# Eight long-convolution products: two channel tiles by turns, one written order for four engines, filter spectra re-indexed through DRAM

## The chip, the core and the metric

One core of a Trainium2 chip runs the kernel. The metric is the device time of one execution in microseconds (us), lower is better. The engines are named as in the profile: PE (matmuls; PEld its weight loads), DVE (VectorE), ACT (ScalarE), POOL (GpSimd), SP (its queue issues most of the DMAs; ACT's queue issues some).

## What is computed

One layer of a hybrid encoder on 2048 tokens of width 1024, in float32. One input projection feeds two mixers. The change is in the first, a gated long convolution over the whole sequence with filters that a small network makes from positions:

```python
def long_conv(z, h_fwd, h_bwd, d_skip):
    L = z.shape[1]
    n = 2 * L
    zf = jnp.fft.rfft(z, n=n, axis=1)
    hf = jnp.fft.rfft(h_fwd, n=n, axis=0) + jnp.conj(jnp.fft.rfft(h_bwd, n=n, axis=0))
    y = jnp.fft.irfft(zf * hf[None], n=n, axis=1)[:, :L]
    return y + z * d_skip

def hyena_mixer(u, ...):
    v, x1, x2 = jnp.split(short_conv3(u, conv_w, conv_b), 3, axis=-1)
    h = hyena_filters(L, ...)
    z = x1 * long_conv(v, h[:, 0, 0], h[:, 0, 1], sk[0])
    z = x2 * long_conv(z, h[:, 1, 0], h[:, 1, 1], sk[1])
    return z
```

There are 512 channels, so four tiles of 128, and two convolutions in series for each: eight products. The second mixer is a recurrence (RWKV-7). Both mixers are then projected, gated and merged, and a dense channel mixer (SwiGLU) follows.

## The kernel before

The stages in order of time: the input projection with the preparation of the recurrence, the recurrence (`chain`, L622) with the rest of the projection beside it, the convolutions (`hyena`, L1230), the merging of the mixers (`merge`, L1470) and the channel mixer (`ffn`, L1619). The change is in `hyena` and in what hands over to it at both ends.

A convolution of a tile of 128 channels goes through an FFT in two steps. `turned` (L1240) transposes the input on PE so that time lies on partitions. `fwd` (L1253) is the first step, matmuls with `Fz` into the tile `U`. `flip` (L1221) swaps indices inside SBUF with four 32x32 block transposes of 128x1024 on DVE, from `U` to `V`. `step3` (L1274) is the second step, matmuls with `Mc` into the PSUM tile `pz`; eight blocks q = 0 to 7 make a tile. For blocks 1 to 7 of the data `parts` (L1264) first splits `V` into a high and a low part `vh` (ACT and DVE), and three float32r matmuls of 512 columns replace the four float32 matmuls of 128. The two lines at L1317 and L1318 then multiply `pz` by the filter's spectrum `H` and by `Hs` (the same with real and imaginary blocks swapped, made by four small DMAs at L1290). `back` (L1297) adds the two products up with eight matmuls (`pq`) and ACT copies them to `Q` (L1304). `flip` turns `Q` into `V` again, `inverse` (L1327) is the last step, `po`. After the first convolution of a tile the result is multiplied by `x1` (L1394) and goes on to `fwd`; after the second `finish` (L1335) transposes it back (`pv`) and gates it with `x2` (L1343).

The filters go the same way: `filt` (L1184) makes, for each of eight blocks, the taps (`pg`, L1206), multiplies them by a window (four ACT exponentials, L1205; DVE, L1210), transforms them (`pf`, L1196) and copies them to `U` (L1197); sixteen pieces of four matmuls per filter. `flip` makes `Vf` of it, and `load` (L1283) its spectrum `H`. `short` (L1157) makes the rows `v`, `x1` and `x2` by a three-tap convolution, in four blocks (ACT L1171, DVE L1172 and L1177).

The eight products run tile by tile (c = 0 to 3), the two of a tile one after the other. PE's order is the order in which the code is written (`manual_schedule` for PE alone); the other engines are ordered by a scheduler, with `high_priority` marks. A product is written as a loop over q in which pieces of the next filter are pulled in (`share`); between two products stand the flips, the inverse, the gate and the next forward transform. After the last product stand the weights of the other mixer's output (`branch_weights`) and seven of its blocks (`right`).

Of the kernel before, what the change touches and what calls it, by code (L numbers as in the profile page):

```python
# [37 lines left out]
TB = 256  # L38

# [149 lines left out]
class Layer:  # L189
# [38 lines left out]
    def build(self):  # L228
        tc, nc = self.tc, self.nc
        with tc.tile_pool(name="dr", bufs=1, space=DRAM) as dr, tc.tile_pool(name="keep", bufs=1, reuse_waits="tile") as keep:  # L230
# [8 lines left out]
            self.Yd = T("Yd", [NCH, P, 256])  # L239
            self.Nd, self.Wd = T("Nd", [2, P, 1024]), T("Wd", [2, P, 1024])  # L240
# [378 lines left out]
    def ring(self, k, n=512):  # L619
        return self.cm.tile([P, 514], F32, name="rg", tag=f"rg{k % 14}")[:, 0:n]  # L620

    def chain(self):  # L622
# [3 lines left out]
        with tc.tile_pool(name="ch", bufs=1, reuse_waits="tile") as s, tc.tile_pool(name="chp", bufs=1, space=PSUM, reuse_waits="tile") as ps:  # L626
# [316 lines left out]

            LAST = N - 3
# [87 lines left out]
            with tc.manual_schedule(engines={mybir.EngineType.PE}):  # L1032
# [17 lines left out]
                taps, pieces = iter(()), [1, 2, 3]  # L1050
                self.rush = 0
                for n in range(N):
# [5 lines left out]
                    if n == LAST + 1:  # L1058
                        taps = self.filt(0, 0)
# [27 lines left out]
                self.taps = taps  # L1087
# [8 lines left out]
    def part(self, gen, need):  # L1096
        while need > 0:
            t = next(gen, None)
            if t is None:
                return  # L1100
            need -= t
            yield t


    def open(self):
# [3 lines left out]
        cu = self.wp.tile([P, 1024], F32, name="cu0", tag="wraw", bufs=2)  # L1109
# [3 lines left out]
        self.turns = dict(cu=0, row=0, w=0, g=0, A=0, B=0, H=0, Hs=0)  # L1113
        self.smalls, self.Vfs = {}, {}
# [4 lines left out]
        self.small(0, 0)  # L1119
        self.taken(0)  # L1120
        self.cus = [cu, self.ring(13, 514)]
        self.z0 = self.short(0, True)
# [12 lines left out]
    def next(self, name):  # L1135
        first, n = dict(w=(8, 2), g=(10, 2), A=(12, 2), B=(0, 2), H=(2, 3), Hs=(5, 3))[name]
# [15 lines left out]
    def row(self):  # L1152
        self.turns["row"] += 1
        return self.cm.tile([P, L], F32, name="co", tag=f"X{1 - self.turns['row'] % 2}")


    def short(self, ct, byrest):  # L1157
        nc, cw, cb = self.nc, self.cw, self.cb
        stt = nc.vector.scalar_tensor_tensor
        o = self.row()  # L1160
        for b in range(NB):
            u = self.cus[self.turns["cu"] % 2]
            self.turns["cu"] += 1
# [5 lines left out]
            nc.sync.dma_start(u[:, lo:hi], self.ud[ct, :, 512 * b - 1 + lo:512 * b - 1 + hi])  # L1169
# [14 lines left out]
    def filt(self, c, o):  # L1184
# [3 lines left out]
        if (c, o) != (HT - 1, 1):  # L1188
            self.small(c + o, 1 - o)
# [530 lines left out]
```

## Time and profile before

| | us |
|---|---|
| median of 3 runs | 3982.31 (3978.8 to 3995.08) |
| the profiled execution | 3993.76, of it 3992.0 from the first to the last instruction |
| projection and recurrence, to PE's last projection matmul | 0 to 1546 |
| end of the recurrence | 1546 to 1600 |
| convolutions, to the last added product | 1600 to 2128 |
| their end, to the first merging matmul | 2128 to 2148 |
| merge and channel mixer | 2148 to 3992 |

A row of the view of stretches gives for each engine the busy time and in brackets the instructions; a float32 matmul of PE is recorded as two. PEclk is the clock that PE was granted, as a share of 2.4 GHz; its other level is 1.2 GHz. In the view of groups, behind the bar stands the idle time of the engine just before the group's instructions, with what ended it.

### The profile page before, as it was taken

What the parts mean: (1) busy time and instruction counts of PE and PEld (TensorE: products, weight loads), DVE (VectorE), ACT (ScalarE), POOL (GpSimd) and SP (SyncE); (2) the same over time, 40 slices, a digit from 0 to 9 for tenths busy, and PEclk for the clock granted to TensorE, in tenths of its full rate; (3) what the DMA queues carried; (4) which work ended last, traced back from release to release, by engine and by line L of the source; (5) the groups of instructions that cost most, each with busy time, mean ns of one, the idle gap of its engine ahead of it and who ended that gap; (6) DMA issues with size and microseconds to landing.
All of it is one profiled execution on the core that took longest, in us unless ns stands there. A gap on an engine that the chain in (4) does not pass through costs nothing. (4 is left out here: it accounts for less than half of the span.)

```text
span 3992.0 us, 64401 instructions
## 1 busy us (share of the span) xinstructions
PE 3822.1 (96%) x25872; PEld 3128.8 (78%) x25872; DVE 2420.1 (61%) x3823; ACT 1488.8 (37%) x2914; POOL 93.1 (2%) x139
## 2 busy tenths in 40 slices
PE   8999999999999998898998999999999999999998
PEld 6766557787787777787887999788888878888887
DVE  4456884666667774878776655544444474444444
ACT  3345663333345567565654332211111151111113
POOL 0000001111010100000000000000000000000000
PEclk9999999999999999899999999999999999999999
DMA  4566878677777775221225433411111132111111
GB/s 139 173 167 172 221 208 245 203 220 208 218 225 224 214 193 178 63 77 46 81 63 176 131 122 117 164 48 48 48 48 48 48 134 78 48 48 48 48 48 43
DMA packets 389554, 501.84 MB, mean 126 GB/s; under 512 B 135220, under 2 KB 270909, under 8 KB 388549
## 3 DMA queue, kind: packets, MB, share of 16 engines
q1 hardware_dynamic: 362631, 443.13, 37.5%
q10 hardware_dynamic: 20736, 37.80, 3.1%
q0 software_dynamic: 5888, 16.78, 1.5%
q8 instruction: 204, 3.34, 0.4%
q14 instruction: 95, 0.78, 0.1%
HBM read 352.74 MB, written 127.93 MB: 120 GB/s over the span
## 5 line engine op out<-in xcount | busy, mean ns | idle before, releaser
L201 PE MATMUL acc<-xh,wh 128*128 128x512 f32 x1376 | 580.2, 422 | 10.3 <-ACT xh L196 9.2
L202 PE MATMUL acc<-xl,wh 128*128 128x512 f32 x1376 | 549.3, 399 | 6.6 <-DVE xl L197 4.9
L203 PE MATMUL acc<-xh,wl 128*128 128x512 f32 x1376 | 548.8, 399 | 0.5 <-DVE wl L197 0.5
L1657 DVE TENSOR_TENSOR acc<-pd,acc 128x1024 f32<-128x1024 f32 x320 | 387.8, 1222 | 70.9 <-PE pd L203 65.1
L196 ACT CAST fwh<-raw 128x1024 fp32r<-128x1024 f32 x132 | 138.6, 1050 | 705.0 <-PE pg L202 488.0
L201 PEld LDWEIGHTS acc<-xh,wh 128*128 128x128 f32 x1376 | 262.9, 191 | 122.9 <-issue 48.2
L1685 DVE TENSOR_TENSOR h<-pu,sg 128x512 f32<-128x512 f32 x88 | 60.9, 692 | 483.1 <-PE pu L203 475.8
L202 PEld LDWEIGHTS acc<-xl,wh 128*128 128x128 f32 x1376 | 263.3, 191 | 65.5 <-DVE xl L197 7.9
L203 PEld LDWEIGHTS acc<-xh,wl 128*128 128x128 f32 x1376 | 262.7, 191 | 65.1 <-issue 1.9
L201 PE MATMUL pd<-fwh,hh 128*128 128x512 f32 x704 | 276.8, 393 | 2.0 <-DVE acc L1655 1.6
L201 PE MATMUL pu<-fxh,fwh 128*128 128x512 f32 x704 | 276.2, 392 | 0.4 <-ACT fxh L1571 0.4
L201 PE MATMUL pg<-fxh,fwh 128*128 128x512 f32 x704 | 276.6, 393 | 0.0
L203 PE MATMUL pg<-fxh,fwl 128*128 128x512 f32 x704 | 275.6, 391 | 0.0
L203 PE MATMUL pd<-fwh,hl 128*128 128x512 f32 x704 | 275.1, 391 | 0.0
L203 PE MATMUL pu<-fxh,fwl 128*128 128x512 f32 x704 | 275.1, 391 | 0.0
L202 PE MATMUL pd<-fwl,hh 128*128 128x512 f32 x704 | 274.7, 390 | 0.0
L202 PE MATMUL pg<-fxl,fwh 128*128 128x512 f32 x704 | 274.4, 390 | 0.0
L202 PE MATMUL pu<-fxl,fwh 128*128 128x512 f32 x704 | 273.7, 389 | 0.0
L197 DVE TENSOR_TENSOR fwl<-raw,fwh 128x1024 fp32r<-128x1024 f32 x132 | 161.3, 1222 | 165.9 <-ACT fwh L196 161.9
L197 DVE TENSOR_TENSOR wl<-wraw,wh 128x512 fp32r<-128x512 f32 (+1 forms) x217 | 169.5, 791 | 144.6 <-ACT wh L196 138.0
L196 ACT CAST wh<-wraw 128x512 fp32r<-128x512 f32 (+1 forms) x217 | 150.3, 704 | 230.2 <-PE acc L202 203.5
L1226 DVE STREAM_TRANSPOSE V<-U 128x1024 f32<-128x1024 f32 x96 | 181.0, 1951 | 30.7 <-ACT U L1304 12.5
(299 smaller groups left out, 7574.4 us busy)
## 6 DMA issues: line engine op xcount, KB each, us to landing
wraw<-in_w_in SPq DMA_DIRECT2D x130, 512.0 KB, 4.5
ABp<-ABd SPq DMA_DIRECT2D x64, 512.0 KB, 5.1
raw<-in_fg SPq DMA_DIRECT2D x44, 512.0 KB, 3.4
raw<-in_fu SPq DMA_DIRECT2D x44, 512.0 KB, 3.4
raw<-in_fd SPq DMA_DIRECT2D x44, 512.0 KB, 3.5
ud<-ev ACTq DMA_DIRECT2D x84, 256.0 KB, 3.1
ABd<-AB SPq DMA_DIRECT2D x32, 512.0 KB, 5.1
gated<-ev SPq DMA_DIRECT2D x64, 256.0 KB, 3.4
```

The source lines that it names most:

```text
L196: nc.scalar.copy(hi, src)
L197: nc.vector.tensor_tensor(out=lo, in0=src, in1=hi.bitcast(F32), op=ALU.subtract)
L201: mm(ps, ah, bh, start=start, stop=False)
L202: mm(ps, ah, bl, start=False, stop=False)
L203: mm(ps, al, bh, start=False, stop=stop)
L1226: self.nc.vector.transpose(V[:, :, sl].rearrange("p j c -> p c j"), U[:, :, sl].rearrange("p n c -> p c n"))
L1657: tt(out=acc[t], in0=pf, in1=acc[t], op=ALU.add)
L1685: tt(out=h, in0=put, in1=sg, op=ALU.mult)
```

## The change

`PRODUCTS` fixes a new order of the eight products, given as (tile, convolution): (0,0) (1,0) (0,1) (1,1) (2,0) (3,0) (2,1) (3,1). While product k runs over its eight blocks, `beside` puts between them the flips of the result of product k-1, its inverse and gate, the forward transform and flips of the data of product k+1, pieces of coming filters (`F`) and blocks of coming rows (`conv`). A product's neighbours belong to the other tile, so a product's own result is needed one product later. `manual_schedule` now holds for PE, ACT, DVE and SP: all four take the order in which the code is written. The split into high and low parts is gone: all blocks go through four float32 matmuls (`second`). The filters are no longer flipped on DVE: ACT copies a transformed block to one of two spots and stores it from its own queue to the DRAM tensor `Hd`, and SP reads it back with the two indices swapped, in two halves, into `Vf` (`given`, for the first half after block 3 and for the second after block 6 of the product before). Windows are computed one piece ahead. The weights of the other mixer's output are split during product 6 and 7, and three of the seven `right` blocks stand in product 7. `norm` takes its two small tiles from tags that exist already. The diff, cut to what the text speaks of:

```diff
+PRODUCTS = [(c + k, o) for c in (0, 2) for o in range(2) for k in range(2)]
+            self.Hd = T("Hd", [2 * HT, 32, P, P])
@@ chain
-                taps, pieces = iter(()), [1, 2, 3]
+                self.taps, pieces = self.filters(), [1, 2, 3]
-                            aux[p].append(self.part(taps, 1.7 if p else 0.8))
+                            aux[p].append(taps(2 if p else 1))
-                for part in (gated(2), channel_major(1), channel_major(0), gated(0)):
+                self.z1 = self.short(1)
+                for part, k in ((gated(2), 2), (channel_major(1), 6), (channel_major(0), 1), (gated(0), 0)):
                     self.pull(part, 1e9)
-                    self.pull(taps, 0.8)
+                    self.pull(taps(k), 1e9)
@@ filters: the end of a piece
-            nc.scalar.copy(U[:, 4 * q:4 * q + 4], p)
+                u = self.spots[q % 2].rearrange("p (a b) -> p a b", b=P)
+                nc.scalar.copy(u, p)
+                nc.scalar.dma_start(self.Hd[i, 4 * q:4 * q + 4].rearrange("n p c -> p n c"), u)
...
-        self.Vfs[c, o] = self.flip(U)
@@ hyena
+                tc.manual_schedule(engines={E.PE, E.Activation, E.DVE, E.SP}):
-                if lo is not None:
-                    self.mm3(p.rearrange("p a b -> p (a b)"), Mh, Ml, hi.rearrange("p a b -> p (a b)"), lo.rearrange("p a b -> p (a b)"), True, True)
-                    return p
+            def given(i, half):
+                self.upto(16 * i + 16)
+                t = s.tile([P, 16, P], F32, name="Vf", tag=f"vf{half}", bufs=1)
+                for k in range(4):
+                    nc.sync.dma_start(t[32 * k:32 * k + 32], self.Hd[i, :, 32 * k + 16 * half:32 * k + 16 * half + 16])
+                Vf[i, half] = t
+            def beside(k, Q):
...
+                if k:
+                    VQ, piece = flips(Q, k + 1)
+                    f = [lambda q=q: piece(q) for q in range(4)]
+                    put(0, f[0], F, F, f[1], F)
+                    put(1, f[2], F, F, f[3], F)
...
+                if k and o == 0:
...
+                    put(1, t[0], t[1])
+                    put(2, t[2], t[3], conv, n[0], n[1])
+                    put(3, n[2], u[0], n[3], conv, u[1])
+                    put(4, u[2], conv, u[3], F)
...
+                if on:
+                    f = [lambda q=q: flipped(q) for q in range(4)]
+                    put(5, f[0], F, F, conv, F)
+                    if k and o:
+                        put(5, g[3])
+                    put(6, f[1], F, F, f[2], F)
...
+                    put(7, f[3], F, conv, F)
+            for k in range(N):
...
+                for q in range(8):
+                    times(k, q, Vs[k])
+                    n, r = divmod(q + 2, 8)
+                    if k + n < N:
+                        load(k + n, r)
+                    if k or q:
+                        added(*((k, q - 1, Qs[k]) if q else (k - 1, 7, Qs[k - 1])))
+                    for f in at[q]:
+                        f()
+                    if q in (3, 6) and k + 1 < N:
+                        given(k + 1, q // 4)
+            added(N - 1, 7, Qs[N - 1])
+            for q in range(4):
+                piece(q)
+                self.right(ps, 3 + q)
```

`t` are the transposes of an input, `n` the inverse with the multiplication by `x1`, `u` the forward step, `f` the flips, `g` the gates.

PE in the joint between the second product of tile 0 and the first of tile 1, in the kernel before (L1259 forward step, L1280 second step, L1332 inverse, L1341 and L1245 transposes):

```order
L1259 MATMUL pfz<-z,Fz 128x128 x32
L1280 MATMUL pz<-V,Mc 128x128 x8
L1332 MATMUL po<-V,Gc 64x128 x16
L1341 MATMUL pv<-k_c_ident,rg 128x128 x4
L1332 MATMUL po<-V,Gc 64x128 x8
L1341 MATMUL pv<-k_c_ident,rg 128x128 x4
L1332 MATMUL po<-V,Gc 64x128 x8
L1341 MATMUL pv<-k_c_ident,rg 128x128 x8
L1245 MATMUL ph<-k_c_ident,co 128x128 x16
```

All of the inverse and the transposes stands in one run, with no block of a product between.

And PE of the changed kernel around blocks 2 and 3 of product 1 (L1309 with `V` the second step of the data, with `Vf` that of the filter two blocks ahead, L1358 inverse, L1294 forward step):

```order
L1285 MATMUL ph<-k_c_ident,co 128x128 x8
L1358 MATMUL po<-V,Gc 64x128 x16
L1309 MATMUL pz<-V,Mc 128x128 x4
L1309 MATMUL pz<-Vf,Mc 128x128 x4
L1348 MATMUL pq<-rg,Mc 128x128
L1349 MATMUL pq<-rg,Mc 128x128
```

Two transposes and sixteen matmuls of the inverse have moved in between two blocks of another product.

DVE at the same joint in the kernel before (L1317 and L1318 multiply, L1226 flips, L1343 gates, L197 is the low part of the split):

```order
L1317 TENSOR_TENSOR rg<-pz,rg 128x512
L1318 TENSOR_TENSOR rg<-pz,rg 128x512
L1226 STREAM_TRANSPOSE V<-U 128x32x32 x8
L1343 TENSOR_TENSOR co<-pv,co 128x8x64 x2
L197 TENSOR_TENSOR vh<-V,vh 128x512 x2
L1343 TENSOR_TENSOR co<-pv,co 128x8x64 x2
```

Eight flips stand in a row here, behind the last multiplication.

And DVE of the changed kernel in the last two blocks of product 0 and the first two of product 1 (L1339 and L1340 multiply, L1303 flips, L1244 multiplies taps by the window, L1184 and L1189 are a block of a row):

```order
L1339 TENSOR_TENSOR rg<-pz,rg 128x512
L1340 TENSOR_TENSOR rg<-pz,rg 128x512
L1303 STREAM_TRANSPOSE V<-U 128x32x32
L1184 SCALAR_TENSOR_TENSOR cv<-cu_16347,k_conv,cv 128x512
L1189 SCALAR_TENSOR_TENSOR co<-cu_16347,k_conv,cv 128x16x32
L1170 MEMSET cu_16347 128x1
L1244 TENSOR_TENSOR rg<-pg,rg 128x512
L1339 TENSOR_TENSOR rg<-pz,rg 128x512
L1340 TENSOR_TENSOR rg<-pz,rg 128x512
L1303 STREAM_TRANSPOSE V<-U 128x32x32
L1244 TENSOR_TENSOR rg<-pg,rg 128x512
L1303 STREAM_TRANSPOSE V<-U 128x32x32
```

Runs of four to eight flips became single flips or pairs between multiplications.

SP of the changed kernel across blocks 3 to 6 of product 0 (L1329 makes `Hs`, L1173 brings a block of a row, L1319 reads a half of a filter back); before, the same queue had only the first two of these:

```order
L1173 DMA cu_16369<-ud 128x514
L1319 DMA Vf<-Hd 32x2048 x4
L1329 DMA rg<-rg 32x512 x4
L1173 DMA cu_16347<-ud 128x514
L1329 DMA rg<-rg 32x512 x4
L1173 DMA cu_16369<-ud 128x513
L1329 DMA rg<-rg 32x512 x4
L1319 DMA Vf<-Hd 32x2048 x4
L1329 DMA rg<-rg 32x512 x4
```

The reads of a filter stand ahead of the small DMAs of the blocks that follow.

## Rows read from the trace of the kernel before

**Rows 1.** The page: busy time of each engine, PE's granted clock by slices.

```profile
PE 3822.1 (96%) x25872; PEld 3128.8 (78%) x25872; DVE 2420.1 (61%) x3823; ACT 1488.8 (37%) x2914; POOL 93.1 (2%) x139
PEclk9999999999999999899999999999999999999999
```

**Rows 2.** Stretches: from:to, length, busy time (instructions) by engine, PEclk, DMA.

```profile
core 0: us, PE busy (x) PEld busy (x) DVE busy (x) ACT busy (x) POOL busy (x), PEclk, DMA share, GB/s
1580.00:1600.00 20.00, 10.36 (x59) 8.77 (x57) 8.56 (x20) 19.80 (x54) 0.00 (x0) 0.74 0.16 48
1600.00:1630.00 30.00, 25.82 (x154) 23.63 (x154) 24.34 (x24) 15.95 (x29) 0.00 (x0) 0.72 0.25 63
1630.00:2128.00 498.00, 443.17 (x3662) 414.44 (x3663) 391.07 (x451) 282.19 (x588) 0.00 (x0) 0.95 0.26 68
```

**Rows 3.** PE's waits from 1546 to 2190, one line: total us, times, longest.

```profile
PE pz L1280 <- DVE V L1226: 16.2, 5, 4.9
```

**Rows 4.** PE in order of time, a joint of two products: start, length, what, idle before.

```profile
1684.05 3.51 PE L1259 MATMUL pfz<-z,Fz 64*128 64x128 f32 x32 [1.30 <-DVE z L1394]
1695.76 2.05 PE L1280 MATMUL pz<-V,Mc 128*128 128x128 f32 x8 [3.06 <-DVE V L1226]
```

**Rows 5.** DVE in order of time at the same joint.

```profile
1688.22 7.39 DVE L1226 STREAM_TRANSPOSE V<-U 128x1024 f32<-128x1024 f32 x4 [3.05 <-ACT U L1261]
```

**Rows 6.** PE back to back at full clock, for the start-to-start time of each form.

```profile
1652.39 0.48 PE L201 MATMUL pz<-vh,Ms 128*128 128x512 f32 x1
...
1653.17 1.05 PE L1196 MATMUL pf<-rg,Fc 128*128 128x128 f32 x8
1654.06 0.39 PE L1302 MATMUL pq<-rg,Mc 128*128 128x128 f32 x2
...
1751.90 1.97 PE L1332 MATMUL po<-V,Gc 128*64 128x128 f32 x32
1753.80 0.66 PE L1341 MATMUL pv<-k_c_ident,rg 128*128 128x128 f32 x4
```

**Rows 7.** Groups of DVE by form, 1600 to 2150: count, busy us, mean ns, idle before.

```profile
L1226 DVE STREAM_TRANSPOSE V<-U 128x1024 f32<-128x1024 f32 x96 | 181.0, 1951 | 30.7 <-ACT U L1304 12.5 <-ACT U L1261 11.2 <-ACT U L1197 7.0
L1317 DVE TENSOR_TENSOR rg<-pz,rg 128x512 f32<-128x512 f32 x64 | 43.9, 687 | 46.9 <-PE pz L203 36.9 <-PE pz L1280 10.0
L1210 DVE TENSOR_TENSOR rg<-pg,rg 128x512 f32<-128x512 f32 x56 | 38.2, 682 | 12.8 <-PE pg L1206 8.0 <-ACT U L1197 3.9 <-issue 0.2
L197 DVE TENSOR_TENSOR vh<-V,vh 128x512 fp32r<-128x512 f32 x56 | 38.0, 684 | 0.6 <-ACT vh L196 0.6
L1177 DVE SCALAR_TENSOR_TENSOR co<-cu,k_conv,cv 128x512 f32<-128x512 f32 x27 | 29.1, 1113 | 0.3
L1172 DVE SCALAR_TENSOR_TENSOR cv<-cu,k_conv,cv 128x512 f32<-128x512 f32 x27 | 19.8, 746 | 5.4 <-ACT cv L1171 5.3
```

**Rows 8.** Groups of ACT by form, 1600 to 2148.

```profile
L196 ACT CAST vh<-V 128x512 fp32r<-128x512 f32 x56 | 33.8, 616 | 31.6 <-DVE V L1226 23.9 <-PE pz L203 6.8
L1197 ACT COPY U<-pf 128x512 f32<-128x512 f32 x58 | 33.5, 577 | 9.3 <-PE pf L1196 9.1
L1171 ACT ACTIVATE cv<-cu,k_conv 128x512 f32<-128x512 f32 x26 | 21.2, 814 | 11.8 <-DMA cu<-ud 11.6
```

**Rows 9.** First multiplication of the first product; last flips (DVE).

```profile
1625.12 0.69 DVE L1317 TENSOR_TENSOR rg<-pz,rg 128x512 f32<-128x512 f32 x1 [0.66 <-PE pz L1280]
...
2129.57 7.58 DVE L1226 STREAM_TRANSPOSE V<-U 128x1024 f32<-128x1024 f32 x4
```

**Rows 10.** PE after the last added product, and the first merging matmul.

```profile
2128.62 0.36 PE L201 MATMUL pr<-y,wh 128*128 128x256 f32 x1
...
2148.18 0.37 PE L201 MATMUL pm<-y,wh 128*128 128x256 f32 x1
```

**Rows 11.** DMA issues: queue, count, KB each, median us to landing.

```profile
rg<-rg SPq DMA_DIRECT2D x256, 64.0 KB, 2.0
yrd<-yo SPq DMA_DIRECT2D x16, 256.0 KB, 3.9
```

More of the change, by code (lines that the diff above doesn't have):

```diff
@@ L614, in prep, with ring @@
                 yield 1.0
[L619 to L620 removed]
+    def ring(self, k):
+        return self.cm.tile([P, 512], F32, name="rg", tag=f"rg{k % 14}")
     def chain(self):
@@ L1177, in short, with filters @@
             stt(out=last, in0=rest, scalar=cw[:, ct, 2:3], in1=t, op0=ALU.mult, op1=ALU.add)
-        return o
+            if b == NB - 1:
+                self.convs[ct] = o
+            given(k + 2)
+            self.blocks = k + 1
+            yield
+    def short(self, ct):
+        while ct not in self.convs:
+            next(self.conv)
+        return self.convs.pop(ct)
     def pre(self, k):
         return self.cm.tile([P, 32, P], F32, name="U", tag=f"G{k % 2}")
-    def filt(self, c, o):
+    def filters(self):
@@ L1216, in filt, with window @@
-        spec(7, last)
-        yield 0.87
-        self.Vfs[c, o] = self.flip(U)
-    def flip(self, U, ahead=0):
-        V = self.hy.tile([P, 32, P], F32, name="V", tag="post", bufs=3)
-        for q in range(4):
-            sl = slice(32 * q, 32 * q + 32)
-            with self.tc.high_priority(offset=ahead):
-                self.nc.vector.transpose(V[:, :, sl].rearrange("p j c -> p c j"), U[:, :, sl].rearrange("p n c -> p c n"))
-        return V
+        ahead = None
+        def window(delta, q):
+            w = self.next("w")
+            for j in range(4):
+                nc.scalar.activation(w[:, j], delta, AF.Exp, scale=self.tcol[:, 4 * q + j:4 * q + j + 1])
+            return w
@@ new lines, in load, with times, added @@
+                hs[i, q] = H, Hs
+            AB = {}
+            def times(i, q, V):
+                p = second(V[:, 4 * q:4 * q + 4], q)
+                H, Hs = hs.pop((i, q))
+                A, B = self.next("A"), self.next("B")
+                tt(out=A, in0=p, in1=H, op=ALU.mult)
+                tt(out=B, in0=p, in1=Hs, op=ALU.mult)
+                AB[i, q] = A, B
+            def added(i, q, Q):
+                A, B = AB.pop((i, q))
+                p = ps.tile([P, 4, P], F32, name="pq", tag="pq")
+                for j in range(4):
+                    m = 0 if 4 * q + j == 0 else 3
+                    mm(p[:, j], Mc[:, m + 1], A[:, j], start=True, stop=False)
+                    mm(p[:, j], Mc[:, m + 2], B[:, j], start=False, stop=True)
+                nc.scalar.copy(Q[:, 4 * q:4 * q + 4], p)
@@ new lines, in back, with gate, outward, result @@
+            def back(v):
+                p = ps.tile([P, 4, P], F32, name="pv", tag="pq")
+                for j in range(4):
+                    nc.tensor.transpose(p[:, j], v[:, j], self.ident)
+                return p
+            def gate(p, x2, q):
+                w = x2.rearrange("p (a b) -> p b a", b=32)[:, 8 * q:8 * q + 8]
+                tt(out=w, in0=p.rearrange("p a (b c) -> p (a b) c", b=2), in1=w, op=ALU.mult)
+            def outward(k, VQ):
+                c = PRODUCTS[k][0]
+                v, ws = zt("x1"), {}
+                def result(q):
+                    p = inverse(VQ, q)
+                    nc.scalar.copy(v[:, 4 * q:4 * q + 4], p)
+                def turned(q):
+                    ws[q] = back(v[:, 4 * q:4 * q + 4])
+                def gated(q):
+                    if q == 0:
+                        ws["x2"] = self.short(2 * HT + c)
+                    gate(ws.pop(q), ws["x2"], q)
+                    if q == 3:
+                        nc.sync.dma_start(self.yhd[c], ws["x2"])
+                return result, turned, gated, ws
```

442 lines of the change are left out of this document (236 added, 206 removed).

## Prediction, made before the changed kernel ran

> **What bounds the kernel now.** I read the page first: PE is busy 96% of the span, at nearly full clock everywhere [rows 1]. A gain must therefore come from PE's own work, or from a stage where PE is not that busy. The page's slices are 100 us wide and hide such a stage, so I read the stretches next [rows 2]. Between 1630 and 2128 PE is busy 443.17 of 498 us, at a granted clock of 0.95; DVE is busy 391 and ACT 282. No engine is full, so PE is held by dependences, not by another engine's load. Ahead of it, from 1600 to 1630, the clock is 0.72, between the two levels of 1.2 and 2.4 GHz; from 1580 to 1600 ACT is busy 19.80 of 20 us, so that this end of the recurrence is paced by ACT.
>
> Next, who holds PE: of its waits in the stage the largest line is the second step waiting for flips, 16.2 us in 5 waits, the longest 4.9 [rows 3]. In order of time one sees it at a joint of two products: the forward step waits 1.30 us for the product with `x1`, and then the second step 3.06 us for the flips [rows 4], since four flips stand in a row on DVE, 7.39 us [rows 5]. While this lasts PE has only filter pieces to do, and those need ACT and DVE too.
>
> **What PE must do.** Prices are start-to-start times at full clock [rows 6]. Eight records (four float32 matmuls) take 1654.06 - 1653.17 = 0.89 us; one fp32r trio 1653.17 - 1652.39 = 0.78; 32 records of the inverse 1.90 to 1.97. A product has 448 records of the 0.89 form or of its size (64 data, 64 filter load, 128 added, 128 filter pieces, 64 forward): 50.2. The inverse is 64 records, 4.0, and 24 transposes at the same price per record come to 2.6. That is 56.8 per product, 454 for eight. Ahead of the first multiplication the changed kernel has done 27 of the filter pieces (24.0), the first transposes and forward step (9.0) and two filter loads (1.8); behind the last added product stand the last inverse and transposes (5.8). Three `right` blocks come in, 1.4 each. So 454 - 40.6 + 4.2 = **418** between the first multiplication and the last added product. The same prices give about 415 for before, where this took 2128.62 - 1625.12 = 503.5 [rows 9, 10]. So 88 us are lost now: 55 are PE not busy [rows 2], the other 33 or so matmuls at the lower clock and seams.
>
> **The change part by part.**
>
> *No split.* 56 trios of 0.78 become 56 quartets of 0.89, +6 us on PE; it is in the 418. DVE loses 56 low parts, 38.0 us [rows 7], ACT 56 casts, 33.8 [rows 8]. Neither is on the path by itself, but the first multiplication of a block follows the flip directly now.
>
> *Filters by DRAM.* DVE loses 32 of 96 flips, 32 x 1.951 = 62.4 us [rows 7]. With the low parts DVE's 391 us fall to about 290 in 440: room, which it had not.
>
> *The order by turns.* The flips of a result and the inverse now have a product of the other tile beside them. What is left is local. In the busiest four blocks of a product (5, 6, 7 and the next 0) DVE has 8 multiplications 5.5, 6 flips 11.7, 6 windows 4.1, 2 blocks of a row 3.7 [rows 7]: 25.0 us. PE has there four blocks of (second step + filter load + added) 3.57 and 11 small pieces 0.89, that is 24.1. The two are level, so PE waits a little, where a multiplication stands behind a flip in the written order. Stepping through the two lists by these durations I get 1.5 us of waiting in a product that ends with the multiplication by `x1` and 3.5 in one with gates; 8 products give 20, and I take **25** with the first, where nothing is ahead. From both sides: 0 if PE's run-ahead in PSUM covers it all, and 8 x 6 x 1.95 = 94 if each of the 6 flips of a product lands on PE in full. I am nearer to the lower end because the 55 us not busy now come from runs of four flips and more, not from single ones [rows 5].
>
> *Clock.* With waits of 1 to 2 us only I assume the upper level throughout, as in the stages behind, where the slices show 9 [rows 1]. If the 0.95 of now stayed, 418 would be some 440; the range holds that.
>
> *The start.* Five more pieces and a block row stand in the end of the recurrence, which ACT paces [rows 2]. Of what is added I count two row blocks at 0.814 and three copies at 0.577 on ACT [rows 8], 3.4 us with no cover; then the first data's flips have windows between them, some 9.8 us instead of the 7.4 of four in a row [rows 5]: +2 to 2.5. The first multiplication was at 1625.12 [rows 9]; I take 1631. Below: -2, since pieces that are done earlier empty the joint behind; above: +8, if the first half filter read arrives late.
>
> *The tail.* From the last added product to the first merging matmul it is 2148.18 - 2128.62 = 19.6 [rows 10]; four flips in 7.58 stand in it [rows 9], with `right` blocks beside them. The changed kernel has the same flips and four `right` blocks: 20.6, give or take 2.
>
> *DMA.* New are 64 stores of 256 KB from ACT's queue and 64 reads of 256 KB on SP's. The nearest row is `yrd<-yo`, a store of 256 KB, 3.9 us; the small ones for `Hs` land in 2.0 [rows 11]. Per product of some 56 us that is 2 MB out and 2 MB back, about 75 GB/s on top of 68 in the stretch, whose DMA share is 0.26 [rows 2]. A half is asked for two to five blocks before its first use (10 to 25 us) and four reads of 3.9, even one after the other, are 15.6; I take it as covered. Without cover each half costs up to 15.6. The issue of 64 stores on ACT costs no more than one small instruction each, and ACT has 282 busy in 498.
>
> **The sum.** 1631 + 418 + 25 + 20.6 = 2094.6 for the first merging matmul, against 2148.2: -54. The stages behind are not touched. The profiled execution takes 3993.76, its changed form some 3940; the median of the runs is 3982.31, 11 lower, so 3982.3 - 54 = **3928**.
>
> **The rivals.**
>
> A. *The stalls hide altogether.* DVE falls to some 290 in 440, and a block's spare PSUM covers single flips. Then 25 becomes 0 to 10: 3903 to 3913, and to 3895 if the start doesn't move. Against it: in the busiest blocks DVE has 25.0 to PE's 24.1.
>
> B. *`Hs` comes late.* The four small DMAs that make `Hs` of a block stand on SP's queue behind 1 MB of filter reads, with 2.0 us when alone [rows 11]. They are asked for two blocks ahead, 8 to 12 us; four reads at 3.9 one after the other are 15.6. Then 3 to 6 us per half, 14 halves, some 45 us at worst: 3973. For it: the order of the queue. Against it: DMA's share of 0.26 [rows 2] leaves reads that overlap. The Trainium skill ("Trainium Kernel Development and Optimization", Key Constraints) says that the queues of different engines share the same 16 DMA engines, so that a read on SP would also meet ACT's stores; no row here shows the two together.
>
> C. *Slower: the written order.* Four engines now stand in a fixed order, and a multiplication that waits for PE holds the flip behind it, which PE needs next; likewise ACT with a `Q` copy ahead of a store. If every one of the 6 flips of a product lands on PE in full, that is 94 instead of 25, and ACT's copies on the same ring (four to eight per product at 0.58 [rows 8]) add 20 to 35: 4015 to 4030. It decides from 54 / 8 = 6.7 us per product above what I assumed. Against it: the hand walk.
>
> D. *Strided DRAM swap.* If runs of 512 bytes slowed the stores well beyond 3.9 us, filters would pace the stage: eight per product must fit into 56 us, so from 7 us each. `yrd<-yo` writes 256 KB in 512-byte runs as well, in 3.9 [rows 11], so I give it little. The rule that speaks against the change is in the Trainium skill ("VectorE: DVE Perf Modes", The three transpose paths): a transpose by a plain DMA with access patterns is given there as some 19 times slower than the transposing DMA. Taken at its word, 19 x 3.9 would be an estimate of 74 us per store, and the sum would end far above 4100; but here only the index between runs is swapped.
>
> E. *No change*: the joints' 55 us return between the blocks and the start eats the rest, near 3982.
>
> **How the numbers follow.** Forecast 65%, with its own range 3905 to 3952 (stalls 5 to 40, start -2 to +8). A 8%, 3890 to 3905. B 14%, 3950 to 3980. C 7%, above 4002. D 2%. E 4%. A measurement can tell about 0.5%, 20 us: the bounds are 3962 and 4002. Faster: the forecast, A and half of B, 0.81 (0.65 + 0.08 + 0.08); same: the rest of B, E and a little of C, 0.12; slower 0.07. Eight in ten lie between 3900 and 3970.
>
> **What would show it.** Right: from the first multiplication to the last added product 440 to 450 instead of 503.5; PE's wait for flips [rows 3] at a few us for single ones under 2; PE's share above 0.93 and clock near 1 in this stretch; no wait for `Vf` or `Hs`; the first multiplication near 1631. Wrong: multiplications that end a wait for a DMA (B); PE's wait for `Q`, `V` or `pz` buffers at every block, with DVE and ACT idle in between (C); pieces waiting for a spot that a store holds (D); a first multiplication after 1640, where ACT's end of the recurrence would have been mis-sized.

## The result, and the profile after

The changed kernel takes 3947.12 us (median of 4 runs, 3939.11 to 3947.99) against 3981.27 of the kernel before on the same chip: a ratio of 0.9903, interval 0.9877 to 0.9929, so 34 us less. It is faster, as forecast, and inside the range of 3905 to 3952, near its upper end; the forecast 54 us were 20 too many. The medians of b_nosplit and a_dma2 in the table take in one execution each far above the others (9865.74 and 4061.09 us), which the ratios leave out.

The profiled execution has a span of 3946.2 us, 45.8 less than that of before. Five marks divide it; the same marks serve for every kernel below. They are the last projection matmul, the first transposes of the convolutions, the first multiplication by a filter, the last added product and the first merging matmul. The table gives the distances between them in us, from the order in time of PE and DVE.

| kernel | median | to first transposes | to first multiplication | to last added product | to first merging | to the end |
|---|---|---|---|---|---|---|
| before | 3981.27 | 51.6 | 27.6 | 503.4 | 19.7 | 1843.8 |
| changed | 3947.12 | 63.1 | 27.8 | 461.5 | 19.7 | 1836.2 |
| b_dram | 4017.90 | 53.4 | 28.7 | 534.6 | 21.9 | 1843.2 |
| b_nosplit | 3993.63 | 52.0 | 27.8 | 514.9 | 21.2 | 1842.4 |
| b_both | 4012.77 | 52.7 | 24.1 | 529.6 | 23.6 | 1842.4 |
| a_pe_only | 3969.87 | 61.9 | 35.9 | 477.2 | 18.7 | 1834.2 |
| a_flip4 | 3961.61 | 64.7 | 27.8 | 482.9 | 19.2 | 1837.7 |
| a_dma2 | 3994.49 | 63.3 | 28.3 | 505.4 | 18.5 | 1838.5 |
| a_pool2 | 3961.92 | 64.4 | 27.8 | 476.0 | 19.3 | 1835.5 |
| a_pool | 3942.86 | 62.0 | 27.8 | 464.7 | 18.4 | 1837.6 |
| a_spread | 4002.59 | 61.5 | 27.7 | 520.2 | 19.4 | 1839.1 |
| a_tail | 3946.59 | 63.9 | 22.6 | 464.2 | 20.0 | 1836.5 |
| a_fewer | 3938.41 | 58.7 | 23.1 | 463.9 | 18.4 | 1835.0 |
| a_best | 3940.34 | 59.2 | 23.2 | 466.9 | 18.5 | 1836.5 |

The first mark itself shows no effect of the change. It stands at 1545.88 in the profile of before and at 1537.92 after, but the three b_ kernels, which have the old code ahead of it, have it at 1532.1 to 1537.9, and all the other profiles between 1527.7 and 1539.9. These 8 us are scatter and account for most of what the two profiles differ by more than the medians. Behind that mark, the change is +11.7 us up to the first multiplication, -41.9 in the products, 0 in the tail and -7.6 in the stages behind: -37.8.

The page of the changed kernel, busy time and PE's granted clock, answering [rows 1], and three stretches, answering [rows 2]:

```profile
PE 3801.3 (96%) x26152; PEld 3128.1 (79%) x26152; DVE 2346.6 (59%) x3734; ACT 1456.8 (37%) x2851; POOL 93.1 (2%) x139
PEclk9999999999999999899999999999999999999999
1580.00:1600.00 20.00, 14.90 (x70) 13.41 (x70) 7.54 (x15) 14.87 (x41) 0.00 (x0) 0.63 0.34 98
1600.00:1629.00 29.00, 26.98 (x180) 24.98 (x181) 13.23 (x12) 17.32 (x41) 0.00 (x0) 0.76 0.55 133
1628.79:2090.26 461.47, 431.57 (x3934) 413.43 (x3933) 326.99 (x373) 249.19 (x518) 0.00 (x0) 0.99 0.52 136
```

The page alone would say that nothing happened: PE is busy 96% in both. The last row is where the gain is. Between the first multiplication and the last added product PE is not busy for 461.5 - 431.6 = 29.9 us, where it was 55, and its granted clock is 0.99 instead of 0.94 to 0.95. Both count. Taking the start-to-start times of PE's records one by one, and as price of a record the mean of its form inside an unbroken group at the upper level, the matmuls of the stage lost 27 us to the lower level before (it was granted in 56 of the 503 us) and 4 us after (10 of 461). So of the 41.9 us by which the stage is shorter, 25 are less waiting and 23 are less time at the lower clock; some 7 us go the other way, mostly at the places where one form of matmul follows another.

PE's waits from 1600 to 2120 in the changed kernel, answering [rows 3] (total us, times, longest), and two groups of DVE from 1600 to 2110, answering [rows 7]:

```profile
PE pz L1309 <- DVE V L1303: 13.6, 7, 5.9
PE po L1358 <- DVE V L1303: 5.9, 2, 4.7
PE pg L1240 <- ACT cu L1228: 4.1, 6, 0.7
PE pz L1309 <- DVE rg L1340: 2.7, 2, 2.4
...
L1303 DVE STREAM_TRANSPOSE V<-U 128x1024 f32<-128x1024 f32 x64 | 143.6, 2248 | 27.0 <-ACT U L1295 14.6 <-ACT U L1350 12.4
L1340 DVE TENSOR_TENSOR rg<-pz,rg 128x512 f32<-128x512 f32 x64 | 43.7, 683 | 11.0 <-DMA rg<-rg 11.0
```

PE still waits for flips, seven times and 0.8 to 5.9 us at a time. DVE waits 11.0 us for `Hs` in nine waits, and no wait of PE ends with one of these: the 2.7 us at `pz` all lie at the joint of products 6 and 7, where the multiplication stands behind flips and not behind a transfer. A flip takes 2.248 us on the average, not 1.951 as in [rows 7].

### The profile page after: what moved, and what is told of

Same layout as the page of the kernel before. It is cut to its first block, busy times and chain, and to the rows that moved or that the text cites. A ratio compares the mean times of both kernels' runs of the same rounds, so it can differ in the third digit from the quotient of the medians.

```text
span 3946.2 us, 64945 instructions
## 1 busy us (share of the span) xinstructions
PE 3801.3 (96%) x26152; PEld 3128.1 (79%) x26152; DVE 2346.6 (59%) x3734; ACT 1456.8 (37%) x2851; POOL 93.1 (2%) x139
## 4 chain that ended last, share of the span: by engine, by line
PE 51%; DVE 3%; DMA 2%; ACT 1%; issue 1%; SPq 0%; ACTq 0%; DVEq 0%
PE pg L205 4%; PE pg L203 4%; PE pu L203 4%; PE pu L204 4%; PE pg L204 4%; PE pu L205 4%; PE pd L203 4%; PE pd L205 4%; PE pd L204 4%; PE pz L1309 2%; PE pm L203 1%; PE pm L204 1%; PE pm L205 1%; PE po L204 1%; PE po L205 1%; PE po L203 1%
## 5 line engine op out<-in xcount | busy, mean ns | idle before, releaser
L1814 DVE TENSOR_TENSOR acc<-pd,acc 128x1024 f32<-128x1024 f32 x320 | 387.6, 1221 | 69.3 <-PE pd L205 63.6
L203 PEld LDWEIGHTS pd<-fwh,hh 128*128 128x128 f32 x704 | 132.0, 188 | 41.0 <-DVE acc L1814 12.2
```

The lines of the kernel that those rows point to most:

```text
L203: mm(ps, ah, bh, start=start, stop=False)
L1814: tt(out=acc[t], in0=pf, in1=acc[t], op=ALU.add)
```

## The experiments

Names with b_ are the kernel before with one part of the change; names with a_ are the changed kernel with one edit. Ratios are to the kernel before on the same chip.

**Which part gains: the parts alone, in the old order.** b_dram replaces the flips of a filter in `filt`:

```diff
+            nc.scalar.dma_start(self.Hd[2 * c + o, 4 * q:4 * q + 4].rearrange("n p c -> p n c"), U[:, 4 * q:4 * q + 4])
-        self.Vfs[c, o] = self.flip(U)
+        V = self.hy.tile([P, 32, P], F32, name="V", tag="post", bufs=3)
+        for h in range(2):
+            for k in range(4):
+                nc.sync.dma_start(V[32 * k:32 * k + 32, 16 * h:16 * h + 16], self.Hd[2 * c + o, :, 32 * k + 16 * h:32 * k + 16 * h + 16])
```

> The kernel before, with one part of the change: a transformed filter block is stored to DRAM by ACT's queue as it is made, and SP reads the whole filter back with swapped indices into the tile that the four flips filled; no filter is flipped on DVE. Order theory (PE waits at the joints for runs of data flips, and those stay): DVE loses 32 flips, some 62 us of its 391, PE's idle time in the stage stays above 45 of 55 us, 3970 to 3988. Load theory (DVE was too full, and its relief is what counts): PE's idle time falls to 30 us or less, 3945 to 3962.

b_nosplit lets `parts` return the block as it is:

```diff
-                k = 4 * (q % 2)
-                hi, lo = room[:, k:k + 4], room[:, k + 8:k + 12]
-                with tc.high_priority(offset=FIRST):
-                    self.split(hi, lo, v)
-                return hi, lo
+                return v, None
```

> The kernel before, with another part of the change: data blocks go through four float32 matmuls, no high and low parts. Order theory: PE gets 56 x 0.11 = 6 us more work, DVE loses 38 us and ACT 34 us, and the joints gain perhaps 1 us each since a block follows its flips directly: 3975 to 3990. Load theory: PE's waits shrink by 15 us or more, 3960 to 3972.

> The kernel before with both parts, filters through DRAM and no split, tile by tile as it was. What the changed kernel gains beyond this one is the order by turns (with the end of the recurrence). Order theory: at most a third of the 34 us that the change gains, 3968 to 3988, with PE idle 40 us or more in the stage. Load theory: two thirds or more, 3940 to 3958.

Measured: b_dram 1.0085 (1.0061 to 1.0110), b_nosplit 1.0032 (1.0015 to 1.0049), b_both 1.0071 (1.0047 to 1.0096). All three are slower than the kernel before, and slower than either theory had allowed for. DVE's busy time in the products falls from 395 to 313 us in b_both, and the stage still grows from 503 to 530. The load theory falls by b_nosplit, where DVE has 34 us less to do and PE's time not busy is 58 us instead of 55; b_dram and b_both cannot test it alone, since they bring new waits of their own. From b_both to the changed kernel it is 66 us. These two differ by the order by turns, the written order of ACT, DVE and SP, the place at which the filters are read back and the end of the recurrence. No run has the order by turns alone.

Why b_dram loses is in its trace. PE's waits (from 1546 to 2230), then SP's queue, DVE and PE in order of time at the first joint:

```profile
PE pz L1286 <- ACT rg L1292: 24.1, 4, 7.6
PE pq L1309 <- DVE rg L1324: 19.9, 3, 6.8
...
1730.90 3.65 SPq L1223 DMA_DIRECT2D V<-Hd  x8
1734.65 25.33 SPq L1296 DMA_DIRECT2D rg<-rg  x7
...
1736.66 0.69 DVE L1323 TENSOR_TENSOR rg<-pz,rg 128x512 f32<-128x512 f32 x1 [1.20 <-PE pz L203]
1744.64 0.69 DVE L1324 TENSOR_TENSOR rg<-pz,rg 128x512 f32<-128x512 f32 x1 [7.28 <-DMA rg<-rg]
1749.40 14.75 DVE L1232 STREAM_TRANSPOSE V<-U 128x1024 f32<-128x1024 f32 x8 [4.06 <-ACT U L1310]
...
1745.39 0.79 PE L1309 MATMUL pq<-rg,Mc 128*128 128x128 f32 x2 [6.75 <-DVE rg L1324]
```

SP issues eight reads at 1730.90, a whole filter at once where the changed kernel asks for half a filter at a time, and the four small transfers that make `Hs` of a block stand right behind them. Such a read lands in 7.1 us (median), in halves it is 4.1. The second multiplication (L1324) waits 7.28 us for that transfer, and PE 6.75 us for the multiplication; the flips behind (eight in a row, 14.75 us) start that much later. The other new wait, 24.1 us, is of PE's second step for ACT's copy to `H`. That this too comes from buffers held until `Hs` has been read is my reading; no run separates it. The wait for `Hs` is the prediction's rival B, in the old order.

**What the written order of the other engines is worth.** a_pe_only:

```diff
-                tc.manual_schedule(engines={E.PE, E.Activation, E.DVE, E.SP}):
+                tc.manual_schedule(engines={E.PE}):
```

> The changed kernel with the written order for PE alone; ACT, DVE and SP are ordered by the scheduler, as in the kernel before. If PE's order carries the gain and the rest follows from it: within 10 us of the changed kernel's 3947. If the written order of DVE and ACT is needed (the scheduler groups flips or puts rows and windows ahead of them): PE's waits for flips grow by 15 us or more, 3962 to 3985. If the written order costs something: 3925 to 3937.

Measured: 0.9967 (0.9954 to 0.9980), 23 us above the changed kernel. The products take 477 us, and the way from the first transposes to the first multiplication 35.9 instead of 27.8. The waits of PE (from 1636 to 2120) are others than expected, not for flips but for windows and for the multiplication with `Hs`:

```profile
PE pg L1240 <- DVE rg L1244: 12.7, 7, 2.9
PE pz L1309 <- DVE rg L1340: 11.9, 7, 6.4
```

So the written order on ACT, DVE and SP, the prediction's rival C, gains 23 us rather than costing anything. That is about a third of the 66 us between b_both and the changed kernel.

**What DVE's room is worth in the new order.** a_flip4 puts the flips that the filters would need back as load:

```diff
+                    if 1 < q < 6:
+                        dm = Qs[k][:, 24:32].rearrange("p a b -> p (a b)").rearrange("p (x y) -> p x y", y=32)
+                        nc.vector.transpose(dm, Vs[k][:, :, 0:32].rearrange("p n c -> p c n"))
```

> The changed kernel with four flips more in each product, one behind each of blocks 2 to 5 on DVE (they write what is written over later): as many as the filters would need on DVE, 32 x 2.25 = 72 us of DVE time. If DVE has room in those blocks, as its 327 busy us of 461 say: 3947 to 3960. If each lands on PE, since the order is fixed and a multiplication stands behind each: half or more of 72, 3983 to 4020. This prices what the path through DRAM is worth inside the new order.

Measured: 0.9952 (0.9933 to 0.9972), 14.5 us above the changed kernel; the products take 482.9 us, 21 more. DVE's busy time grew by 56 us, so a quarter to two fifths of it reaches the end, between the two expectations. To spare DVE the flips of the filters is worth 15 to 20 us in the new order (15 by the medians, 20 by the ratios); in the old order the same path, with a whole filter read at once, costs 36. With these flips back on DVE the new order is still 21 us faster than the kernel before, which is the nearest that a run comes to the order without this part.

**How near rival B is.** a_dma2 issues each read of a filter twice on SP's queue, a_pool issues the reads once from POOL's queue, a_pool2 twice from there:

```diff
-                for k in range(4):
+                for k in (0, 1, 2, 3, 0, 1, 2, 3):
-                    nc.sync.dma_start(t[32 * k:32 * k + 32], self.Hd[i, :, 32 * k + 16 * half:32 * k + 16 * half + 16])
+                    nc.gpsimd.dma_start(t[32 * k:32 * k + 32], self.Hd[i, :, 32 * k + 16 * half:32 * k + 16 * half + 16])
```

(a_dma2 has the first pair of lines, a_pool the second, a_pool2 both.)

> The changed kernel with each read of a filter from DRAM issued twice, 128 reads of 256 KB instead of 64, on the same queue: 1 MB more ahead of the Hs transfers at each half. If the reads are covered with room to spare: within 8 us of 3947. If the rival of the prediction (Hs late behind the reads) is near: DVE's waits for Hs, 11.0 us in 9 waits in the profile of the changed kernel, grow to 40 us or more and the time to 3962 to 3995.

> The changed kernel with the 64 reads of filters issued from POOL's queue instead of SP's; the same bytes at the same places in the program, but the Hs transfers stand behind no read. If the order on SP's queue makes Hs late: DVE's 11.0 us of waiting for Hs fall under 4, the stage shortens by 2 to 8 us, 3939 to 3945. If it is the shared transfer engines, or if POOL's queue is slower to issue: 11 us stay or grow, 3946 to 3965.

> The same with every read issued twice, from POOL's queue, as the run with doubled reads did from SP's, which made the time 3994.5 and the stage 505 us. If those 44 us came from Hs standing behind the reads on SP's queue: under 3960. If they came from the bytes, and the transfer engines are what is short: 3975 or more. Waits for the filter itself (9.5 us there, in 3 waits) should stay in either case, since the doubled reads still stand ahead of it.

Measured: a_dma2 1.0028 (1.0011 to 1.0046), 47 us above the changed kernel; a_pool 0.9906 (0.9887 to 0.9926), 4 us below it, which these runs cannot tell from none; a_pool2 0.9949 (0.9931 to 0.9967), 15 above. The waits in a_dma2, of DVE and then of PE, and PE's in a_pool2:

```profile
DVE rg L1340 <- DMA rg<-rg: 45.2, 10, 7.7
PE pz L1309 <- DVE rg L1340: 15.7, 5, 4.1
PE pz L1309 <- DMA Vf<-Hd: 9.5, 3, 4.6
...
PE pz L1309 <- DMA Vf<-Hd: 14.7, 3, 12.0
PE pz L1309 <- DVE rg L1340: 3.7, 2, 2.4
```

With the doubled reads ahead of it on the same queue, `Hs` makes DVE wait 45.2 instead of 11.0 us, and the stage is as long as before the change. But it is not 1 MB more of transfers alone that stands ahead. The second read of a pair writes where the first one writes, and SP waits until the first has landed (56 waits, 69.3 us in all). The reads of one half on SP's queue, first in the changed kernel and then in a_dma2:

```profile
1713.36 1.77 SPq L1319 DMA_DIRECT2D Vf<-Hd  x4
...
1712.21 8.91 SPq L1319 DMA_DIRECT2D Vf<-Hd  x8
```

Four reads occupy the queue for 1.77 us, eight for 8.91, and the transfers for `Hs` are issued only then. The same doubled reads from another queue cost 15 us against the changed kernel and 19 against a_pool, and what is left there is mainly the filter itself coming late. So most of the price is the place in SP's queue, which stands still, and not the bytes. The bytes show as well: the transfers for `Hs` land in 3.3 us (median) in a_pool2, and in 2.0 before [rows 11]. The Trainium skill ("Trainium Kernel Development and Optimization", Key Constraints) has the queues share 16 DMA engines; the 15 us of a_pool2 do not speak against it, but the queue's order was the larger part here. With single reads from POOL's queue, where they are also issued earlier, DVE has no wait for `Hs` left, and the stage is 464.7 us as against 461.5: the 11.0 us of the changed kernel were hidden.

a_spread leaves the reads on SP's queue, and spreads the four of a half:

```diff
+                    if q in (3, 4, 5, 6, 7) and k + 1 < N:
+                        read(k + 1, q // 6, {3: (0, 1), 4: (2,), 5: (3,), 6: (0, 1), 7: (2, 3)}[q])
```

> The changed kernel with the four reads of a half spread over the blocks on SP's queue: two behind block 3, one behind 4 and 5, two behind 6 and 7, instead of four behind 3 and four behind 6. Queue theory: Hs waits for at most two reads, DVE's 11.0 us fall to 5 or less, 3939 to 3945. Rival: the wait on SP for the last store to land is what holds Hs, not the reads, or the last read now comes late itself: 3946 to 3962.

Measured: 1.0051 (1.0032 to 1.0069), 55 us above the changed kernel. One line of PE's waits (from 1610 to 2120) holds the whole of it:

```profile
PE pz L1309 <- DMA Vf<-Hd: 54.8, 7, 9.4
```

The last read of the first half stood behind block 5, and block 6 uses it: 7.8 us of waiting for each of seven filters, since the read is issued 4.8 to 5.8 us before the matmul that ends the wait. In the changed kernel two whole blocks lie between, the last read of a half is issued 6.9 us or more before its first use, and PE never waits for a filter. The edit was badly chosen to test the queue, but it measures the lead that the swap needs: no block between is too little, and two suffice. What one would do no run shows.

**The joint of products 6 and 7.** It has the longest waits of the changed kernel. PE, DVE and ACT there, in order of time:

```profile
2044.46 2.05 PE L1309 MATMUL pz<-V,Mc 128*128 128x128 f32 x8 [5.86 <-DVE V L1303]
2057.15 1.16 PE L1309 MATMUL pz<-Vf,Mc 128*128 128x128 f32 x8 [2.38 <-DVE rg L1340]
...
2042.13 2.18 DVE L1303 STREAM_TRANSPOSE V<-U 128x1024 f32<-128x1024 f32 x1
2050.96 4.39 DVE L1303 STREAM_TRANSPOSE V<-U 128x1024 f32<-128x1024 f32 x2 [2.65 <-ACT U L1350]
...
2038.58 0.62 ACT L198 CAST wh<-wr 128x512 fp32r<-128x512 f32 x1 [2.98 <-DMA wr<-in_w_rw]
```

The weights of the other mixer are split between these flips, and ACT waits for their load. a_tail moves all eight splits into product 7, and one of the three `right` blocks from there to the last flips:

```diff
-        for dt, q in enumerate((5, 6, 6, 7, 7)):
-            at[q].append(lambda dt=dt: self.weights_on(dt))
...
+        for dt, q in enumerate((1, 2, 2, 3, 4, 5, 5, 6)):
+            at[q].append(lambda dt=dt: self.weights_on(dt))
```

> The changed kernel with the other mixer's weights split in product 7 instead of from the end of product 6 on, and two right blocks in product 7 instead of three (the third goes between the last flips). At the joint of products 6 and 7 PE waits 5.86, 2.38 and 1.28 us and loses clock. Theory that the weight splits stand between the flips there on DVE, and ACT's casts wait for their loads ahead of copies that PE needs: the three waits fall to under 4 us together, 3937 to 3942. Rival, eight flips of 2.25 us against five blocks of PE without any filter piece hold PE there alone: waits within 2 us of now, 3945 to 3953.

Measured: 0.9916 (0.9891 to 0.9941), 3946.59, no difference. PE's waits for flips in all the products are 12.5 instead of 13.6, and a new one of 6.0 has come in (PE `pq` for DVE's L1339). At the joint the three waits are 4.58, 1.75 and 1.28 us instead of 5.86, 2.38 and 1.28. The rival holds: no filter piece is left there to fill PE, and the flips pace it, with at most 1.9 us due to the splits.

**The end of the recurrence.** PE there in the changed kernel:

```profile
1588.44 2.07 PE L1226 MATMUL pf<-rg,Fc 128*128 128x128 f32 x8 [2.65 <-ACT cu L1228]
1591.85 2.05 PE L1226 MATMUL pf<-rg,Fc 128*128 128x128 f32 x8 [1.33 <-DVE rg L1244]
...
1594.98 3.35 PE L1240 MATMUL pg<-fw,H3b 128*128 128x128 f32 x14
1598.12 0.42 PE L880 MATMUL pgt<-k_c_ident,y 128*128 128x128 f32 x2
...
1601.02 1.04 PE L1285 MATMUL ph<-k_c_ident,co 128*128 128x128 f32 x8
...
1586.50 1.42 ACT L872 ACTIVATE y<-y,nm,vr 128x64 f32<-128x64 f32 x4
...
1599.27 0.70 ACT L891 ACTIVATE yo<-pgt,k_gn_b,k_gn_w 128x64 f32<-128x64 f32 x2 [4.45 <-DVE yo L889]
```

The recurrence's last output is there at 1587.9 (first row of ACT), but PE transposes it at 1598.12, since six filter pieces stand ahead in its order, partly at the lower clock and three of them behind a wait for ACT or DVE. ACT itself waits 4.45 us there for what comes of the transposes. From the last projection matmul the output is there after 50.0 us (47.3 before) and the transposes begin after 60.2 (46.7 before). a_fewer takes three of them away:

```diff
-                for part, k in ((gated(2), 2), (channel_major(1), 6), (channel_major(0), 1), (gated(0), 0)):
+                for part, k in ((gated(2), 2), (channel_major(1), 3), (channel_major(0), 1), (gated(0), 0)):
```

> The changed kernel with three filter pieces instead of six behind the second-last transposes of the recurrence; the three left out come later, in the first product. The first transposes of the convolutions stand 63.1 us behind the last projection matmul, 51.6 in the kernel before. Theory that the pieces hold PE there (14 matmuls in a row at the lower clock, each window waiting for ACT): 63.1 falls to 54 to 58, the stage grows by 2 to 3 us, 3939 to 3944. Rival, ACT paces this end whatever PE does: 61 us or more, 3944 to 3952.

Measured: 0.9899 (0.9872 to 0.9926), 3938.41. The first transposes of the convolutions come at +58.7 instead of 63.1, and the products take 2.4 us more for the pieces that moved. That is the first theory, a little short. The first multiplication comes another 4.7 us sooner, but this is not the edit's doing: a_tail, which has the changed kernel's code there, has it too (22.6 us in the table). It is the clock. The last half of the first forward step, in the changed kernel and then in a_tail:

```profile
1609.97 5.84 PE L1294 MATMUL pfz<-z,Fz 64*128 64x128 f32 x32
...
1603.17 3.54 PE L1294 MATMUL pfz<-z,Fz 64*128 64x128 f32 x32
```

In the changed kernel these run at the lower level, which was granted from 1605.0 to 1618.7; in a_tail and a_fewer the upper level holds from 1594.9 and 1593.9 on, about the start of this step. So 4.4 of the 11.7 us lost at this end come back by the three pieces. By the medians a_fewer is 9 us below the changed kernel, with ratios whose intervals overlap. a_best adds a_pool's edit to it:

> The changed kernel with two edits together: three filter pieces instead of six in the end of the recurrence (3938 by itself) and the filter reads on POOL's queue (3943 by itself, not told apart from the changed kernel). If the two add up: 3932 to 3937. If the reads' place does nothing that PE sees, as its unchanged stage of 465 us says: 3937 to 3941. If the first half of the first filter comes late because fewer pieces are done before it is read: above 3943.

Measured: 0.9905 (0.9889 to 0.9922), 3940.34; the reads' queue adds nothing that can be told.

## Why the prediction was right, and where its sum was off

**The mechanism held.** Flips, inverse and gates of one tile beside the products of the other: PE's time not busy in the products went from 55 to 29.9 us (25 were forecast), the granted clock from 0.94 to 0.99 (the upper level throughout was assumed), and no product waits for a filter. The gain comes with the order: the two other parts without it (b_both) lose 31 us, and the order with the flips' load put back (a_flip4) still gains 21. Of what the order gives, 23 us hang on its being written for ACT, DVE and SP too (a_pe_only); that the rest is the turns of two tiles is argued, since no run has them alone. Not every sign came as written: the stage takes 461.5 us where 440 to 450 were given, two waits for flips are above 2 us (5.86 and 2.91), and DVE does end nine waits for a transfer, the sign of rival B, without PE waiting for it.

**The work of PE was mis-sized: 418 forecast, 431.6 busy.** This is the largest error, 13.6 of 18.5 us that the stage is longer than forecast. The count of records and their prices held: at the mean start-to-start time of its own form the work of the stage comes to 415 us, 3 less than forecast. What failed is the step that set this sum of start-to-start times beside PE's time not busy, with no term for what lies between the two; seams it named only as part of what is lost now. PE in order of time in the changed kernel:

```profile
1790.85 1.06 PE L1226 MATMUL pf<-rg,Fc 128*128 128x128 f32 x8
1791.74 1.06 PE L1240 MATMUL pg<-fw,H3b 128*128 128x128 f32 x8
1792.63 1.10 PE L1226 MATMUL pf<-rg,Fc 128*128 128x128 f32 x8
1793.58 1.06 PE L1309 MATMUL pz<-V,Mc 128*128 128x128 f32 x8
...
1804.43 1.06 PE L1226 MATMUL pf<-rg,Fc 128*128 128x128 f32 x8
1806.16 1.16 PE L1240 MATMUL pg<-fw,H3b 128*128 128x128 f32 x8 [0.68 <-ACT cu L1228]
1807.16 1.06 PE L1309 MATMUL pz<-V,Mc 128*128 128x128 f32 x8
```

Two groups of pieces follow each other in 0.89 us, as in the sum, and from a piece to the second step it is 0.95. But a group that is followed by a wait counts as busy for its full 1.06 us: from 1804.43 to 1806.16 it is 0.89 for the work, 0.17 for its end and 0.68 not busy. Summed over the stage by start-to-start times, the ends before 42 waits are 7.0 us, 352 places where one form follows another 5.6, and the lower clock 3.9. So a wait costs more than its idle time, by half of what was missing here.

**The waits, 25 forecast and 29.9 found,** have about the right size and a different place. They were spread evenly over eight products; a fifth of them is the one wait of 5.86 us at the joint of products 6 and 7, which has no pieces. A term in them was wrong: flips were priced at 1.95 us, their mean in the kernel before, and take 2.25 in the changed one, 64 x 0.30 = 19 us more on DVE.

**The start, +6 forecast, +11.7 found.** The step counted what ACT gains in work, 3.4 us, and that term held: the recurrence's last output is 2.7 us later. What it left out is PE's order, which holds the last transposes for another 10.2 us behind six pieces, where before they followed at once. a_fewer shows 4.4 us of it with three pieces fewer; the rest is argued from the order of the rows. That the first multiplication stands at 1628.79, near the forecast 1631, is luck: the last projection matmul happened to be 8 us earlier.

**The tail,** +1 forecast, 0 found. **The stages behind** were taken as untouched and are 7.6 us shorter, in the other direction. Together: -54 forecast, +18.5 + 5.7 - 1 - 7.6 off, -38 in the profile, -34 by the medians. That 7.6 us from stages that the prediction held for untouched cover a part of the error is luck as well.

**The parts.** "No split" and "filters by DRAM" were treated as relief for DVE. For the filters that relief is worth 15 to 20 us in the new order (a_flip4); in the old order the parts alone cost 11 and 36 us, and what "no split" is worth in the new order no run shows. The prediction had a mechanism of the loss as rival B, `Hs` behind the reads on SP, with 14 in 100. The place was right, as b_dram and a_dma2 show. Its size was not worked out rightly: 14 halves of 3 to 6 us are 42 to 84, so that its 45 us "at worst" are the low end of its own terms. That a_dma2 comes to 47 us is chance, since there SP waits for reads to land, which is not in the rival. In the changed kernel four reads occupy the queue for 1.77 us, and the 11.0 us that DVE waits are hidden. The rule on transposes by strided DMA ("VectorE: DVE Perf Modes", The three transpose paths, in the Trainium skill) does not bite here, and the Trainium skill itself ties it to a large innermost stride of the destination, where this swap keeps whole runs: the stores of 256 KB land in 2.3 to 2.7 us and the reads in 4.1, near the 3.9 of [rows 11] that the sum used. DMA issues of a_fewer in the products (KB each, median us to landing):

```profile
Vf<-Hd SPq DMA_DIRECT2D x56, 256.0 KB, 4.1
Hd<-cu ACTq DMA_DIRECT2D x25, 256.0 KB, 2.3
Hd<-rg ACTq DMA_DIRECT2D x25, 256.0 KB, 2.7
```

## What to carry to other kernels

A chain of transforms gains when its serial steps stand beside another tile's work, as here, and relieving the engine that PE waits for can gain nothing if that engine was waiting itself: look at who waits in which joint, not at busy shares. When a transfer is put on a queue, price what stands behind it there, ask whether the queue itself will wait, and measure its lead. When PE's work is summed from start-to-start times, add a term for each wait (here 0.17 us) and one for the clock, and look at what is placed ahead of the last step of a latency-bound end. Before a shorter time between two marks is put down to an edit, look for a kernel without the edit that has it too.

## What the runs showed of the hardware

**A stage that the change does not touch got faster.** From the first merging matmul to the end it takes 1842.4 to 1843.8 us in the four kernels with the old convolutions, and 1834.2 to 1839.1 in the ten with the new ones. It is not waits: PE has 8684 records there in either kernel and is not busy for 27.9 us before and 29.1 after. A part of it is matmuls of the channel mixer; groups of PE in the last 1300 us but 50, of before and then of the changed kernel:

```profile
L201 PE MATMUL pg<-fxh,fwh 128*128 128x512 f32 x615 | 241.1, 392 | 0.0
L203 PE MATMUL pg<-fxh,fwl 128*128 128x512 f32 x615 | 240.4, 391 | 0.0
...
L203 PE MATMUL pg<-fxh,fwh 128*128 128x512 f32 x616 | 239.8, 389 | 0.0
L205 PE MATMUL pg<-fxh,fwl 128*128 128x512 f32 x616 | 239.9, 389 | 0.0
```

These two forms have a mean of 392 and 391 ns in one kernel and 389 in the other, with the same code, a granted clock of 1.00 in both stretches and no waits. Why stays open: no run was made on it.

**The flips take longer in the changed kernel, alone or in a run.** It is 1.95 us in the mean before and 2.25 after, with the same 128x1024 elements and the same steps between them. That they now stand alone is not the reason: in the kernel before, 23 flips stand between other instructions and take 1.98. One of these, and the 32 flips that a_flip4 adds, each by itself, in a kernel whose other flips take 2252 ns:

```profile
1664.24 1.96 DVE L1226 STREAM_TRANSPOSE V<-U 128x1024 f32<-128x1024 f32 x1
...
L1516 DVE STREAM_TRANSPOSE U<-V 128x1024 f32<-128x1024 f32 x32 | 62.8, 1961 | 0.1
```

The added flips write without gaps, the others with a step. What makes the changed kernel's own flips longer stays open.
